# A decoder layer in split fp32: copies, sums, loads and stores of the hidden work put at other places in the engines' orders

## The chip, the cores and the metric

The kernel runs on one core of one Trainium2 chip. The core has TensorE (PE in the profile; its weight loads are PEld), VectorE (DVE), ScalarE (ACT), GpSimd (POOL) and SyncE (SP), and 16 DMA engines that move what SP and POOL issue here. The metric is the device time of one execution in microseconds. A time is given as the median of the executions shown.

## The reference, cut to what matters

One post-norm layer, 1024 tokens (S), width 2048, everything float32:

```
h = x @ w_in + b_in
q, k, v, g_attn, u_pool, g_pool = split(h)
a = banded_sink_attention(q, k, v, ...) * silu(g_attn)        # 16 heads, window 128
b = multiscale_pool(u_pool, w_pool, pool_scale) * silu(g_pool)  # trailing means of 2, 4, 8, 16
mix = concat([a, b]) @ w_out
ple = sigmoid(x @ w_gate_ple) * (p_i @ w_ple)
out = layer_norm(sqrt(2) * x + mix + ple, gain, bias)
```

## The kernel before, in words

**Products.** All activations are kept transposed, channels on partitions and tokens along the row. Each float32 operand is split into a high and a low part, `hi` and `lo`, and a product is the sum of hi·hi (L182), hi·lo (L183) and lo·hi (L184). A weight job makes two output blocks of 128 channels over half of the contraction. It is done after Strassen and Winograd, with seven products p1 to p7 in place of eight; their moving operands are the quarters `b11`, `b21`, `b22` of the activations and the sums `t1` to `t4` of quarters, each in a high (`t1h`) and a low (`t1l`) part. One product is 12 matmuls of 128x128 on 128x512: four slices of the contraction, three matmuls each. A product is one *tick* of the kernel's clock.

**Around a product.** SP loads the raw weights (`raw<-in_win`, L139). DVE forms sums of them (`s<-raw`, `raw<-raw,raw`, L125), ACT casts the high part (`wh`, L736), DVE subtracts to get the low part (`wl`, L125). PE leaves the product in a PSUM bank: `qa` or `qb` with two buffers each for a job by itself, `sc` and others for jobs side by side. ACT copies the first product of a quarter into the SBUF buffer of the output block, `part` (L402), DVE adds the others (`part<-part,qb`, L125); both free the bank for a later product. A second half of the contraction adds the first half's result to `part` by an accumulating DMA that POOL issues (L415: `part<-h`, `part<-g`), and some ticks later the block's outcome is worked out (`finished`, `done`).

**Stages**, from the trace of before: the qkv projection's first half with, in the *Head*, early products of the PLE weights ("per-layer embedding") between (to about 120 us); the other first halves with the attention heads woven in (to about 685); the second halves, first the pooling inputs `u` and gates, then the PLE gate `wgate`, then the gates of attention, the last two jobs side by side (to about 1125); the output projection (to about 1280); the same with its columns' mean taken out, for 768 tokens with products of 128x384 (to about 1402); the last 256 tokens without Strassen (to about 1455); the norm's end.

**What sets the order.** The program is written by a Python class. `after(n, fn)` runs `fn` n ticks later; `later(n, fn)` does the same and asks that its instructions be put behind those last issued (`issue_after`). A scheduler with priorities then fixes one order for each engine. Each engine runs its own order strictly: an instruction that waits holds all behind it. SP's loads and stores stand in one order too, and so do POOL's.

**What the change touches.**

- `ple_half` (L778), the PLE products in the Head: eight small groups of matmuls into the banks `tr` and `pv` (one buffer each), then two copies by ACT into `ple_out` (through `copy`, L736; the trace names the buffer `b22h`). `in_turn` asks that copies come behind the one before, once `turn["ACT"]` is set. `early` (L1152) places these halves in the first group.
- `set_from`'s `s2` (L317), which makes the sums `t1`, `t2` of the Head on DVE (`two<-two,two`, 128x1024).
- `set_kept`'s `step` (L344): splits an operand that was kept from the first stage, four pieces, and fetches the one after the next.
- `pool_sums` (L356): from four loaded quarters of the pooled channels (`s<-cc`, 256 KB each) DVE makes `t1`, `t3`, `t2`, `t4` (`s<-s,s`), which POOL stores for the output projection. Four such steps lie in the stage of `wgate`.
- `pool_u` (L704): fetch and split of the pooling's map. `embed_w` (L812): fetch and split of a block of `w_ple`; its high parts are the casts at L153.
- `gate_ahead` (L661) loads the stored attention result of a block (`s<-pre`, two of 256 KB); `gate_attn` (L664) takes the silu on ACT (L666), multiplies by those on DVE (`part<-s,part`), and stores the outcome to `cc` through POOL (`aside`, L144). Four jobs: two by themselves (`s3[-4]`, `s3[-3]`), the last two side by side.
- `job.wait`: the ticks between a block's accumulating DMA and its `done`. In the stage of 768 tokens `done` runs `norm_square`: ACT squares (L921), sums for the norm on PE (L930, L937).
- `norm_scale` (L940; ACT at L954) and `norm_out`, the norm of the 768 tokens, during the last stage.

Code that is quoted below has the line numbers of before. In the changed kernel L736 is L758, L402 is L420, L415 is L433, L666 is L684 and L834 is L857.

Of the kernel before, what the change touches and what calls it, by code (L numbers as in the profile page):

```python
# [64 lines left out]
class Layer:  # L65
# [203 lines left out]
    def set_from(self, get, F, keep=None, first=None, by=None):  # L269

        nc = self.nc
        r = {}

        def fetch(u, part=None):
            h, k = int(u[2]) - 1, 2 * (int(u[1]) - 1)
            if not part:
                r[u] = [self.two() for _ in range(2)]
            for i, t in enumerate(r[u]):
                src = get(h, k + i)
                if part is None:  # L280
                    (by or (nc.sync if first else nc.scalar)).dma_start(out=t, in_=src)
                elif i == 0 and part < 2:
                    self.load(t[:, part], src[:, part])
                elif i == 1 and part == 2:
                    self.load(t, src)

        def sub(u, a, b, place):
            out = []
            for k in range(2):
                o = r[place][k] if place else self.two()  # L290
                self.tt(o, r[a][k], r[b][k], ALU.subtract)
                if keep:
                    self.load(keep[u][k], o)
                out.append(o)
            r[u] = out

        split = lambda u: self.split_unit(u, r[u])

        def begin():
            self.F = F  # L300
            if first:
                first(fetch, r)
                return
            for i, u in enumerate(("b11", "b21", "b12", "b22")):
# [12 lines left out]
        def s2():  # L317
            split("t1")
            sub("t2", "b22", "t1", None if keep else "t1")

        def s3():
            split("t2")
            sub("t3", "b22", "b12", "b12")

        def s4():
            split("t3")
            sub("t4", "b21", "t2", "b21")

        return [begin, s0, s1, s2, s3, s4, lambda: split("b22"), lambda: split("t4")]

    def set_kept(self, get, keep):

        r = {}

        def fetch(i):
            if i < 7:
                u = UNITS[BESIDE[i]]
                h, k = int(u[2:] or 1) - 1, 2 * (int(u[1]) - 1)
                r[u] = []
                for n in range(2):  # L340
                    src = keep[u][n] if u in keep else get(h, k + n)
                    r[u] += [self.fetch(src[:, m]) for m in range(2)]

        def step(i):  # L344
            u = UNITS[BESIDE[i]]
            self.split_unit(u, r.pop(u))
            fetch(i + 2)

        def begin():
            self.F = T  # L350
            fetch(0)
            fetch(1)

        return [begin] + [lambda i=i: step(i) for i in range(7)]

    def pool_sums(self, i, m, keep):  # L356

        at = [(4 + i, 0), (4 + i, 1), (6 + i, 0), (6 + i, 1)]
        r = []

        def make():
            b11, b12, b21, b22 = r
            self.tt(b11, b12, b11, ALU.subtract)
            self.tt(b12, b22, b12, ALU.subtract)
            self.tt(b22, b22, b11, ALU.subtract)
            self.tt(b21, b21, b22, ALU.subtract)
            for u, t in (("t1", b11), ("t3", b12), ("t2", b22), ("t4", b21)):
                self.aside(keep[u][i][:, m], t)

        self.after(2, lambda: r.extend(self.fetch(self.cc[k][:, m, h * T : h * T + T]) for k, h in at))  # L370
        self.later(4, make)

    def set_by_twos(self, get, keep):

# [289 lines left out]
    def gate_attn(self, j, c):  # L664
        nc = self.nc
        nc.scalar.activation(c, c, AF.Silu, bias=self.c(C_BIN + GA0 + j))  # L666
        for h, pre in enumerate(self.got.pop(("ga", j))):
            self.tt(c[:, h], pre, c[:, h], ALU.mult)
        self.aside(self.cc[j // 2][:, j % 2], c.rearrange("p h t -> p (h t)"))

    def gate_pool(self, j, c):
        nc = self.nc
# [4 lines left out]
    def pool_u(self, j, c):  # L677
# [23 lines left out]
        self.diff[j] = out  # L701
        if j % 2:
            f = slice((g % 2) * T, (g % 2) * T + T)
            self.after(4, lambda: self.got.update({("wp", g): self.fetch(self.wpool[g // 2][:, f])}))  # L704
            self.later(8, lambda: self.got.update({("wp", g): self.split(self.got["wp", g])}))
            late = 3 if g == 1 else 0
            self.after(6 + late, lambda: self.got.update({("sg", g): [[self.fetch(self.sgp[2 * g + e][:, h * T : h * T + T]) for e in range(2)] for h in range(2)]}))
            self.later(10 + late // 2, lambda: self.mix(g))
# [69 lines left out]
    def ple_half(self, n, h, tags):  # L778
# [13 lines left out]
        for b in range(2):  # L792
            if h:
                self.aside(self.ple[2 * i + b], self.ple_out[(2 * n + b) % 4].rearrange("p h t -> p (h t)"))

    def embed_in(self, r=None):
        if not r:
# [14 lines left out]
    def embed_w(self, i):  # L812
# [2 lines left out]

        if i not in EARLY:
            r = self.fetch(self.wple[i // 2][:, (i % 2) * T : (i % 2) * T + T])
            self.later(2, lambda: make(r))

    def embed(self, j, c):  # L820
        nc = self.nc
# [166 lines left out]
    def run(self):  # L988
# [47 lines left out]
        def consume(w):  # L1036
            def done(b, c):
# [4 lines left out]
                elif b >= U0:  # L1042
                    self.pool_u(b - U0, c)
                else:
                    self.gate_attn(b - GA0, c)
            return done

        def jobs(todo, half, first, done, tokens=2 * T, ahead=None):
# [4 lines left out]
        s2 += jobs(rest, 1, lambda w: None, lambda w: keep(store(w)))  # L1053
        s3 = jobs(rest, 0, lambda w: kept_part(store(w)), consume)
        for j in s3:
            j.wait = 3 if j in s3[-2:] else 4
            j.ahead = self.embed_ahead if j.w is wgate else (lambda b: self.gate_ahead(b - GA0)) if j is s3[-3] else None
        mixed = [(wout, *p) for p in pairs(0, 8)]
        centred = [(self.wc, *p) for p in pairs(4, 6) + pairs(0, 2)]
        s4 = jobs(mixed, 1, lambda w: kept_part(self.r), lambda w: lambda b, c: self.co_done(b, c))  # L1060
# [4 lines left out]
            j.filled = True  # L1065
        s6 = [Job(w, b0, b1, 0, None, lambda b, c: self.second_done(b, c), F2, plain=True) for w, b0, b1 in centred]
        s6[-1].mean = True
        for j in s4[-2:]:
            j.wait = 6
        self.add(*s1[:3])  # L1070
        self.add(*s1[3:])
# [134 lines left out]
        for i in range(n3):  # L1206
# [7 lines left out]
            if i == n3 - 2:  # L1214
# [202 lines left out]
```

## Time and profile before

| | us |
|---|---|
| median of 3 runs | 1468.27 (1466.94 to 1468.92) |
| the profiled execution's own time | 1470.93 |
| its span | 1469.2 |
| PE busy | 1437.4 (98%) |
| DVE busy | 1120.8 (76%) |
| ACT busy | 787.3 (54%) |
| POOL busy | 294.4 (20%) |
| DMA | mean 205 GB/s over the span, 301.35 MB |

The granted clock of TensorE is 0.996 of full speed over the span. A row of the timeline gives the start in us, the busy time in us, engine, source line, operation and tiles, and in brackets how long the engine was idle ahead of it and what ended that wait. In the trace SP's DMA queue is called SPq. Buffers that share a name share a row.

### The profile page before, as it was taken

To read this page: it belongs to the slowest core of one execution; us is meant where nothing else is said; L and a number is where in the kernel's file an instruction comes from. 1 tells how busy PE (TensorE), PEld (TensorE's weight loads), DVE (VectorE), ACT (ScalarE), POOL (GpSimd) and SP (SyncE) were. 2 spreads that over 40 slices of the span, in tenths; PEclk is the share of its full clock that TensorE was granted. 3 is DMA by queue.
4 is the path that set the end of the run, shared out by engine and by line. 5 is a ranking of instruction groups with operands and counts; after the bars stand their busy time and mean duration, and the time that the engine had idled before them with its cause. 6 is when DMAs were issued, how large, how long until landed. Compare 5 with 4: busy or idle time off the path is not lost. (4 is left out here: it accounts for less than half of the span.)

```text
span 1469.2 us, 20535 instructions
## 1 busy us (share of the span) xinstructions
PE 1437.4 (98%) x6930; PEld 1214.9 (83%) x6930; DVE 1120.8 (76%) x2031; ACT 787.3 (54%) x1564; POOL 294.4 (20%) x416
## 2 busy tenths in 40 slices
PE   9999999999999999999999999999999999999996
PEld 7788888888888888887887788788877788899996
DVE  6869578878788797888668785867678566987786
ACT  6546376565575665566545444333456333554475
POOL 1000203332233333223010111211011111111223
PEclk9999999999999999999999999999999999999998
DMA  9463875554456554557765669899698678595475
GB/s 354 173 241 117 244 216 177 178 167 151 138 179 213 188 172 165 186 180 265 191 190 149 166 179 320 260 288 275 189 335 278 184 179 232 134 263 124 120 243 200
DMA packets 109993, 301.35 MB, mean 205 GB/s; under 512 B 12544, under 2 KB 18048, under 8 KB 109888
## 3 DMA queue, kind: packets, MB, share of 16 engines
q1 hardware_dynamic: 84672, 217.46, 43.4%
q0 software_dynamic: 21888, 75.25, 21.2%
q10 hardware_dynamic: 3328, 7.34, 1.5%
q8 instruction: 54, 0.88, 0.2%
q14 instruction: 51, 0.42, 0.1%
HBM read 205.62 MB, written 94.37 MB: 204 GB/s over the span
## 5 line engine op out<-in xcount | busy, mean ns | idle before, releaser
L736 ACT CAST wh<-raw 128x512 fp32r<-128x512 f32 x428 | 263.9, 619 | 400.5 <-PE qa L183 125.6
L125 DVE TENSOR_TENSOR wl<-raw,wh 128x512 fp32r<-128x512 f32 x428 | 300.0, 704 | 102.7 <-ACT wh L736 97.6
L402 ACT COPY part<-qa 128x512 f32<-128x512 f32 (+1 forms) x180 | 103.7, 576 | 74.9 <-PE qa L184 74.4
L620 POOL TENSOR_SCALAR_AFFINE_SELECT s<-s 128x512 fp32r<-128x512 f32 x128 | 102.4, 812 | 132.0 <-ACT s L613 96.5
L125 DVE TENSOR_TENSOR part<-part,qb 128x512 f32<-128x512 f32 (+1 forms) x120 | 81.1, 676 | 44.7 <-PE qb L184 40.1
L182 PE MATMUL qa<-b11h,wh 128*128 128x512 f32 (+2 forms) x292 | 109.4, 375 | 0.4 <-ACT wh L736 0.4
L182 PE MATMUL qb<-b21h,wh 128*128 128x512 f32 (+2 forms) x292 | 109.3, 374 | 0.0
L184 PE MATMUL qa<-b11h,wl 128*128 128x512 f32 (+2 forms) x292 | 108.8, 373 | 0.0
L184 PE MATMUL qb<-b21h,wl 128*128 128x512 f32 (+2 forms) x292 | 108.8, 372 | 0.0
L183 PE MATMUL qa<-b11l,wh 128*128 128x512 f32 (+2 forms) x292 | 108.7, 372 | 0.0
L183 PE MATMUL qb<-b21l,wh 128*128 128x512 f32 (+2 forms) x292 | 108.6, 372 | 0.0
L182 PE MATMUL qb<-t1h,wh 128*128 128x512 f32 (+1 forms) x260 | 100.8, 388 | 3.4 <-DVE part L125 1.6
L182 PE MATMUL qa<-t2h,wh 128*128 128x512 f32 (+1 forms) x260 | 101.1, 389 | 3.0 <-ACT wh L736 1.8
L182 PE MATMUL qa<-t4h,wh 128*128 128x512 f32 (+1 forms) x260 | 100.7, 387 | 2.7 <-DVE part L125 2.7
L182 PE MATMUL qa<-t3h,wh 128*128 128x512 f32 (+1 forms) x260 | 100.6, 387 | 1.6 <-ACT part L402 1.6
L184 PE MATMUL qa<-t2h,wl 128*128 128x512 f32 (+1 forms) x260 | 100.1, 385 | 1.8 <-DVE wl L125 1.8
L182 PE MATMUL qb<-b22h,wh 128*128 128x512 f32 (+1 forms) x260 | 100.5, 386 | 0.5 <-ACT part L402 0.5
L183 PE MATMUL qa<-t3l,wh 128*128 128x512 f32 (+1 forms) x260 | 99.8, 384 | 0.0
L184 PE MATMUL qb<-t1h,wl 128*128 128x512 f32 (+1 forms) x260 | 99.7, 384 | 0.0
L184 PE MATMUL qa<-t4h,wl 128*128 128x512 f32 (+1 forms) x260 | 99.7, 384 | 0.0
L183 PE MATMUL qa<-t2l,wh 128*128 128x512 f32 (+1 forms) x260 | 99.7, 383 | 0.0
L184 PE MATMUL qb<-b22h,wl 128*128 128x512 f32 (+1 forms) x260 | 99.7, 383 | 0.0
(327 smaller groups left out, 3567.2 us busy)
## 6 DMA issues: line engine op xcount, KB each, us to landing
raw<-in_win SPq DMA_DIRECT2D x65, 512.0 KB, 4.3
h<-part SPq DMA_DIRECT2D x34, 512.0 KB, 2.9
part<-h POOLq DMA_DIRECT2D x34, 512.0 KB, 6.6
cw<-in_wout SPq DMA_DIRECT2D x64, 256.0 KB, 3.0
raw<-in_wgate SPq DMA_DIRECT2D x32, 512.0 KB, 4.4
raw<-wc SPq DMA_DIRECT2D x32, 512.0 KB, 4.3
s<-in_x SPq DMA_DIRECT2D x44, 256.0 KB, 5.9
wc<-cw SPq DMA_DIRECT2D x32, 256.0 KB, 2.4
```

Source lines behind the costliest of these rows:

```text
L125: return (eng or self.nc.vector).tensor_tensor(out=out, in0=a, in1=b, op=op)
L182: mm(ps, wh, xh, start=start, stop=False, skip_group_check=True)
L183: mm(ps, wh, xl, start=False, stop=False, skip_group_check=True)
L184: return mm(ps, wl, xh, start=False, stop=stop, skip_group_check=True)
L402: self.mark("ACT", self.nc.scalar.copy(out=dst, in_=ps))
L620: nc.gpsimd.affine_select(out=o4, in_=a4, pattern=[[0, 4], [sign, P]], compare_op=ALU.is_ge, fill=0.0, base=0 if side else -1, channel_mul ...
L736: ins = self.nc.scalar.copy(out=out, in_=a)
```

## The change

It consists of these parts, in the order of the diff:

- Head: the sum `t2` is made two ticks later, by `later`; in `early` the copies of one half are no longer tied to those before (`turn["ACT"]` is dropped at (2, 1) and set again at (2, 0) from `ple_half`'s return value).
- `set_kept`: from the second step on, two of the four pieces are split one tick later.
- `pool_sums`: `later(4)` becomes two halves at `later(7)` and `later(8)`.
- `pool_u`: the fetch one tick sooner, the split one later. `embed_w`: the split at `later(4)` for `later(2)`.
- Gates: for the jobs `s3[-4]` and `s3[-3]` the loads of `pre` are placed by hand 1, 1, 5 and 6 ticks after the begin of the stage's last part, `wait` is 5 for 4, and the outcome is stored by SP one tick after it is made (`soon`), where POOL stored it at once.
- The squares of the stage of 768 tokens (but for its last two jobs): `wait` 6 for 4. `norm_scale` and `norm_out`: one tick later.

```
         def s2():
             split("t1")
-            sub("t2", "b22", "t1", None if keep else "t1")
+            if first:
+                self.later(2, lambda: sub("t2", "b22", "t1", None))
+            else:
+                sub("t2", "b22", "t1", None if keep else "t1")
...
-            self.split_unit(u, r.pop(u))
-            fetch(i + 2)
+            pieces = r.pop(u)
+            self.split_unit(u, [])
+            for n in range(2):
+                self.split_part(u, n, pieces[n])
+
+            def rest():
+                for n in range(2, 4):
+                    self.split_part(u, n, pieces[n])
+                fetch(i + 2)
+
+            if i:
+                self.after(1, rest)
+            else:
+                rest()
...
         self.after(2, lambda: r.extend(self.fetch(self.cc[k][:, m, h * T : h * T + T]) for k, h in at))
-        self.later(4, make)
+        for second in range(2):
+            self.later(7 + second, lambda second=second: make(second))
...
-        self.aside(self.cc[j // 2][:, j % 2], c.rearrange("p h t -> p (h t)"))
+        store = lambda by: by(self.cc[j // 2][:, j % 2], c.rearrange("p h t -> p (h t)"))
+        if soon:
+            self.after(1, lambda: store(self.load))
+        else:
+            store(self.aside)
...
-            self.after(4, lambda: self.got.update({("wp", g): self.fetch(self.wpool[g // 2][:, f])}))
-            self.later(8, lambda: self.got.update({("wp", g): self.split(self.got["wp", g])}))
+            self.after(3, lambda: self.got.update({("wp", g): self.fetch(self.wpool[g // 2][:, f])}))
+            self.later(9, lambda: self.got.update({("wp", g): self.split(self.got["wp", g])}))
...
-            self.later(2, lambda: make(r))
+            self.later(4, lambda: make(r))
...
-            j.wait = 3 if j in s3[-2:] else 4
-            j.ahead = self.embed_ahead if j.w is wgate else (lambda b: self.gate_ahead(b - GA0)) if j is s3[-3] else None
+            j.wait = 3 if j in s3[-2:] else 5 if j in s3[-4:-2] else 4
+            j.ahead = self.embed_ahead if j.w is wgate else None
...
-        for j in s4[-2:]:
+        for j in s4[-2:] + s5[:-2]:
             j.wait = 6
...
+            if at == (2, 1):
+                self.turn.pop("ACT")
             if at in turn:
-                self.ple_half(*turn[at], (("tr", 1), ("pv", 1)))
+                out = self.ple_half(*turn[at], (("tr", 1), ("pv", 1)))
+                if at == (2, 0):
+                    self.turn["ACT"] = out
...
-                for b in s3[-4].b:
-                    self.after(1, lambda b=b: self.gate_ahead(b - GA0))
+                for n, b in enumerate(s3[-4].b + s3[-3].b):
+                    self.after((1, 1, 5, 6)[n], lambda b=b: self.gate_ahead(b - GA0))
...
-        self.later(3, lambda: self.norm_scale(one, 2))
+        self.later(3, lambda: self.norm_scale(one, 3))
         for j in range(NB):
-            self.later(6 + 18 * j // 16, lambda j=j: self.norm_out(one, j))
+            self.later(7 + 17 * j // 16, lambda j=j: self.norm_out(one, j))
```

First place: ScalarE in the Head, where the copies `b22h<-tr` and `b22h<-pv` free the banks of the PLE products, `t2h` is the cast of a sum for a later operand, and `wh` are weights' high parts. Before:

```order
L736 CAST t1h_521<-two_309 128x1024
L736 CAST t2h_614<-two_527 128x1024
L736 CAST wh_557<-s_208_552 128x512
L736 CAST t2h_614<-two_530 128x1024
L736 COPY b22h_341<-tr_598 128x512
L736 COPY b22h_341<-pv_599 128x512
L736 CAST wh_580<-s_212_575 128x512
L736 CAST wh_624<-raw_293 128x512
L736 CAST wh_660<-raw_295 128x512
L402 COPY part_452<-qb_628 128x512
L736 COPY b22h_341<-tr_642 128x512
```

After:

```order
L758 CAST t1h_521<-two_309 128x1024
L758 CAST wh_551<-s_206_546 128x512
L758 COPY b22h_341<-tr_598 128x512
L758 COPY b22h_341<-pv_599 128x512
L758 CAST t2h_614<-two_569 128x1024
L758 CAST wh_580<-s_212_575 128x512
L758 CAST t2h_614<-two_572 128x1024
L758 CAST wh_624<-raw_293 128x512
L420 COPY part_452<-qb_628 128x512
L758 CAST wh_660<-raw_295 128x512
L758 COPY b22h_341<-tr_642 128x512
```

Both casts of `t2h` moved behind the copies of the first PLE half (`tr_598`, `pv_599`), and one of them behind the cast `wh_580`; the copy of the next half (`tr_642`) still stands behind both.

Second place: VectorE in the stage of `wgate`, around the first step of the pooling's sums. `s_9165<-s_9119,s_9164` is the low part of a `w_ple` block, `s_9168`, `s_9170`, `s_9172` and `s_9174` (`s_9164`, `s_9166` and so on after) are the four loaded quarters, and the additions `part<-part,qb` and `part<-part,qa` free banks. Before:

```order
L125 TENSOR_TENSOR part_9124<-part_9124,qb_9150 128x512
L125 TENSOR_TENSOR s_9165<-s_9119,s_9164 128x512
L125 TENSOR_TENSOR wl_9177<-raw_8652,wh_9176 128x512
L125 TENSOR_TENSOR wl_9200<-raw_8809,wh_9199 128x512
L125 TENSOR_TENSOR s_9168<-s_9170,s_9168 128x512
L125 TENSOR_TENSOR part_8957<-part_8957,s_9106 128x512
L834 SCALAR_TENSOR_TENSOR part_8957<-s_9102,part_8957 128x512
L125 TENSOR_TENSOR s_9170<-s_9174,s_9170 128x512
L125 TENSOR_TENSOR wl_9230<-raw_8833,wh_9229 128x512
L125 TENSOR_TENSOR s_9174<-s_9174,s_9168 128x512
L125 TENSOR_TENSOR s_9172<-s_9172,s_9174 128x512
L125 TENSOR_TENSOR part_9125<-part_9125,qa_9130 128x512
```

After:

```order
L125 TENSOR_TENSOR part_9124<-part_9124,qb_9150 128x512
L125 TENSOR_TENSOR wl_9173<-raw_8652,wh_9172 128x512
L125 TENSOR_TENSOR wl_9196<-raw_8809,wh_9195 128x512
L125 TENSOR_TENSOR part_8957<-part_8957,s_9106 128x512
L857 SCALAR_TENSOR_TENSOR part_8957<-s_9102,part_8957 128x512
L125 TENSOR_TENSOR wl_9222<-raw_8833,wh_9221 128x512
L125 TENSOR_TENSOR s_9216<-s_9119,s_9215 128x512
L125 TENSOR_TENSOR part_9125<-part_9125,qa_9130 128x512
...
L125 TENSOR_TENSOR s_9164<-s_9166,s_9164 128x512
L125 TENSOR_TENSOR raw_8833<-raw_8833 128x512
L125 TENSOR_TENSOR wl_9268<-raw_8833,wh_9267 128x512
L125 TENSOR_TENSOR e_9295<-s_9077,e_9294 128x512
```

The first sum of quarters (`s_9168<-s_9170,s_9168` before, `s_9164<-s_9166,s_9164` after) now stands ten rows behind the addition out of `qa` (`part_9125<-part_9125,qa_9130`); before, it stood seven rows ahead of it.

Third place: SP's queue at the gates of attention. `s<-pre` are the gates' inputs, `two<-pt` and `two<-cc` operands of the next stage, `raw` weights, `cc_236` and `cc_237` the outcome of the two single jobs. Before:

```order
L139 DMA raw_10544<-in_wout 128x1024
L139 DMA two_10580<-pt_252 128x1024
L139 DMA two_10582<-pt_253 128x1024
L139 DMA s_10602<-pre_156 128x512
L139 DMA s_10604<-pre_156 128x512
L139 DMA s_10607<-pre_157 128x512
L139 DMA s_10609<-pre_157 128x512
L139 DMA s_10778<-pre_158 128x512
```

After:

```order
L139 DMA raw_10536<-in_wout 128x1024
L139 DMA s_10561<-pre_156 128x512
L139 DMA s_10563<-pre_156 128x512
L139 DMA cc_236<-part_10290 128x1024
L139 DMA cc_236<-part_10291 128x1024
L139 DMA s_10584<-pre_157 128x512
L139 DMA s_10586<-pre_157 128x512
L139 DMA two_10588<-pt_252 128x1024
L139 DMA two_10590<-pt_253 128x1024
L139 DMA s_10778<-pre_158 128x512
```

The inputs of blocks 156 and 157 moved ahead of the loads of `pt`, and the stores of `cc_236`, which stood in POOL's queue, now stand between them; those of `cc_237` stand ten rows behind them in the same queue, ahead of `two<-pt_256`.

More of the change, by code (lines that the diff above doesn't have):

```diff
@@ L359, in pool_sums, with make @@
         r = []
-        def make():
+        def make(second):
             b11, b12, b21, b22 = r
[L363 to L367, printed above, removed]
+            if second:
+                self.tt(b22, b22, b11, ALU.subtract)
+                self.tt(b21, b21, b22, ALU.subtract)
+            else:
+                self.tt(b11, b12, b11, ALU.subtract)
+                self.tt(b12, b22, b12, ALU.subtract)
+            for u, t in (("t2", b22), ("t4", b21)) if second else (("t1", b11), ("t3", b12)):
                 self.aside(keep[u][i][:, m], t)
         self.after(2, lambda: r.extend(self.fetch(self.cc[k][:, m, h * T : h * T + T]) for k, h in at))
-        self.later(4, make)
+        for second in range(2):
+            self.later(7 + second, lambda second=second: make(second))
     def set_by_twos(self, get, keep):
@@ L662, in gate_ahead, with gate_attn @@
         self.got["ga", j] = [self.fetch(self.pre[j][:, h * T : h * T + T]) for h in range(2)]
-    def gate_attn(self, j, c):
+    def gate_attn(self, j, c, soon):
         nc = self.nc
@@ L668, in gate_attn @@
             self.tt(c[:, h], pre, c[:, h], ALU.mult)
-        self.aside(self.cc[j // 2][:, j % 2], c.rearrange("p h t -> p (h t)"))
+        store = lambda by: by(self.cc[j // 2][:, j % 2], c.rearrange("p h t -> p (h t)"))
+        if soon:
+            self.after(1, lambda: store(self.load))
+        else:
+            store(self.aside)
     def gate_pool(self, j, c):
@@ L794, in ple_half @@
                 self.aside(self.ple[2 * i + b], self.ple_out[(2 * n + b) % 4].rearrange("p h t -> p (h t)"))
+        return out.ins
     def embed_in(self, r=None):
@@ L1044, in done @@
                 else:
-                    self.gate_attn(b - GA0, c)
+                    self.gate_attn(b - GA0, c, b in s3[-4].b + s3[-3].b)
             return done
```

## The prediction

> **What bounds the kernel now.** I read the page first, then the waits of PE, then PE's timeline wait by wait, and for each wait the timelines of ACT and DVE around it. The page's first row and the two longest kinds of wait:
>
> ```profile
> PE 1437.4 (98%) x6930; PEld 1214.9 (83%) x6930; DVE 1120.8 (76%) x2031; ACT 787.3 (54%) x1564; POOL 294.4 (20%) x416
> ```
> ```profile
> PE qa L182 <- ACT part L402: 2.7, 5, 1.2
> PE qa L182 <- DVE part L125: 2.7, 4, 1.7
> ```
>
> PE is the bound. The change takes no matmul away, so all that it can gain is waiting, and few waits are longer than 0.3 us. What one costs shows in the Head:
>
> ```profile
> 38.28 0.39 PE L183 MATMUL qb<-t1l,wh 128*128 128x512 f32 x1
> 38.51 0.39 PE L184 MATMUL qb<-t1h,wl 128*128 128x512 f32 x1
> 40.34 0.50 PE L182 MATMUL tr<-t4h,t3h 128*128 128x512 f32 x1 [1.44 <-ACT b22h L736]
> 40.68 0.40 PE L183 MATMUL tr<-t4l,t3h 128*128 128x512 f32 x1
> ```
>
> Matmuls start 0.23 apart; around this wait the starts are 1.83 and 0.34 apart, so it costs 1.83 + 0.34 - 0.46 = 1.71, the idle time plus 0.27. I price every wait so. A product of 12 matmuls takes 12 x 0.23 = 2.7.
>
> **The change part by part.** *Head.* The wait just shown is for the copy that empties `tr`; the product before it waited for an addition that stood behind the first sum for `t2` on DVE:
>
> ```profile
> 35.93 0.47 PE L182 MATMUL qb<-t1h,wh 128*128 128x512 f32 x1 [0.38 <-DVE part L125]
> ```
> ```profile
> 38.75 1.04 ACT L736 CAST t2h<-two 128x1024 fp32r<-128x1024 f32 x1 [1.64 <-DVE two L125]
> 39.70 0.58 ACT L736 COPY b22h<-tr 128x512 f32<-128x512 f32 x1
> 40.18 0.59 ACT L736 COPY b22h<-pv 128x512 f32<-128x512 f32 x1
> 41.22 0.62 ACT L736 CAST wh<-s 128x512 fp32r<-128x512 f32 x1 [0.45 <-DVE s L125]
> 41.74 1.14 ACT L736 CAST wh<-raw 128x512 fp32r<-128x512 f32 x2
> 42.79 0.57 ACT L402 COPY part<-qb 128x512 f32<-128x512 f32 x1
> 43.26 0.58 ACT L736 COPY b22h<-tr 128x512 f32<-128x512 f32 x1
> ```
> ```profile
> 40.44 0.69 DVE L125 TENSOR_TENSOR s<-raw 128x512 f32<-128x512 f32 x1
> ```
>
> With the copy ahead of both casts of `t2h`, both waits go: 0.65 + 1.71 = 2.4. But the casts now stand ahead of the next copy. Before, the next PLE half would start a half and a product after 40.34, at about 40.34 + 0.1 + 2 x 2.7 = 45.9; with 2.4 taken off, PE wants `tr` at 43.5. On DVE the sum at 40.44 keeps its place (as many rows of the same kind stand ahead of it), ending at 41.1; behind it ACT has a `wh` (0.52 to the next start), `t2h` (0.95), `wh` (0.52), the copy of `part` (0.47), `wh` (0.52) and the copy of `tr` (0.58): it ends at 41.2 + 3.6 = 44.8. So a wait of 1.3 takes the place of those removed, and the Head gains 2.4 - 1.4 = 1.0. Ends: 0 (PE waits as long, one product later) and 2.4 (the copy is in time).
>
> *`set_kept`.* PE's wait ends when a cast of `wh` and an addition end together:
>
> ```profile
> 695.60 0.46 PE L182 MATMUL qb<-t1h,wh 128*128 128x512 f32 x1 [0.89 <-ACT wh L736]
> ```
> ```profile
> 694.77 0.68 DVE L125 TENSOR_TENSOR part<-part,qb 128x512 f32<-128x512 f32 x1
> ```
>
> Each stands one instruction earlier on its engine, which is 0.6: gain 0.6, from 0 to 0.9. Where the same split comes elsewhere, and for `pool_u`'s pieces, no wait of PE stands behind it: nothing; PE's cover is the products already split, and uncovered each would cost one such 0.6.
>
> *Pooling's sums and `w_ple`'s splits.* DVE holds additions behind sums whose quarters have not landed (the rows of DVE), and PE waits four times there, once for ACT behind a sigmoid (the last row):
>
> ```profile
> 916.67 0.69 DVE L125 TENSOR_TENSOR s<-s,s 128x512 f32<-128x512 f32 x1 [4.22 <-DMA s<-cc]
> ...
> 942.87 2.15 DVE L125 TENSOR_TENSOR s<-s,s 128x512 f32<-128x512 f32 x3 [1.22 <-DMA s<-cc]
> ```
> ```profile
> 917.19 0.50 PE L182 MATMUL qb<-b22h,wh 128*128 128x512 f32 x1 [0.46 <-ACT part L402]
> ...
> 921.88 0.50 PE L182 MATMUL qa<-t4h,wh 128*128 128x512 f32 x1 [1.65 <-DVE part L125]
> ...
> 930.57 0.50 PE L182 MATMUL qa<-t2h,wh 128*128 128x512 f32 x1 [0.24 <-ACT part L402]
> ...
> 946.27 0.51 PE L182 MATMUL sc<-e,s 128*128 128x512 f32 x1 [1.68 <-DVE part L125]
> ```
> ```profile
> 915.08 1.06 ACT L822 ACTIVATE part<-part 128x1024 f32<-128x1024 f32 x1 [1.92 <-DMA part<-g]
> ```
>
> The sums come three and four ticks later, 8 to 11 us, which is longer than the wait of 4.22. The waits at 921.88 and 946.27 go (1.92 + 1.95), and that at 930.57, behind casts that are moved, too (0.51): 4.4. The first, 0.46, stays: its copy stands behind a sigmoid that waits for the accumulating DMA `part<-g`, which the change does not bring forward. What is late next is that DMA. On POOL the stores of the sums now come behind later accumulations, and on SP the loads of the quarters keep their tick, so the slots of four quarters are held three ticks longer and loads of `s<-in_x` behind them in SP's order may wait. I find no user on PE within a product of them: 0, with 2.0 to lose (one such wait more) and 0.7 to gain.
>
> *Gates.*
>
> ```profile
> 1077.29 2.66 DVE L125 TENSOR_TENSOR part<-s,part 128x512 f32<-128x512 f32 x4 [3.62 <-DMA s<-pre]
> ...
> 1096.08 0.69 DVE L125 TENSOR_TENSOR part<-s,part 128x512 f32<-128x512 f32 x1 [0.59 <-DMA s<-pre]
> ```
> ```profile
> 1081.20 0.50 PE L182 MATMUL qa<-t4h,wh 128*128 128x512 f32 x1 [0.54 <-DVE part L125]
> ...
> 1099.07 0.49 PE L184 MATMUL qa<-t2h,wl 128*128 128x512 f32 x1 [0.69 <-DVE wl L125]
> ...
> 1108.65 0.50 PE L182 MATMUL qa<-t3h,wh 128*128 128x512 f32 x1 [1.21 <-ACT part L402]
> ```
> ```profile
> 1105.63 0.59 ACT L402 COPY part<-qb 128x512 f32<-128x512 f32 x1 [2.52 <-DMA cc<-part]
> 1106.12 1.99 ACT L736 CAST t1h<-two 128x1024 fp32r<-128x1024 f32 x2
> 1108.01 0.59 ACT L402 COPY part<-qa 128x512 f32<-128x512 f32 x1
> ```
> ```profile
> two<-pt SPq DMA_DIRECT2D x7, 512.0 KB, 8.0
> ...
> cc<-part POOLq DMA_DIRECT2D x4, 512.0 KB, 8.2
> r<-part SPq DMA_DIRECT2D x2, 512.0 KB, 4.4
> ```
>
> With `s<-pre` there, and the silus a tick later, DVE does not stop at 1077, and the first two waits go: 0.81 + 0.96. The third stays, since it hangs on a store: the copy of `part` needs the buffer that `cc` is written from. The multiplications then end at about 1096.1 (the second without its wait of 0.59); SP stores at that time, where POOL stored an instruction later. Landing takes 8.2: 1104.3. Behind it ACT has the copy (0.59), one `t1h` (0.95), a `wh` (0.62) and the copy of `part` out of `qa` (0.59): PE goes on at about 1107.0 instead of 1108.65. The stage's gain is then 1.7; at least 0.8 (the first wait alone) and at most 3.3 (all three). A store on SP also holds SP's queue until DVE is done: `two<-pt` stands behind it. Its first user is ACT's `t2h`, several products later. POOL's accumulations `part<-h`, which stood behind those stores, now wait for their own data alone; I count nothing for it, as the silu of a tick later finds them landed either way.
>
> The Trainium skill says in DMA: Bandwidth & Descriptors, section "Issuing engines are not separate DMA queues", that DMAs of all issuers run on the same engines, and another issuer saves only the small time of initiation; the trace agrees (POOL's 8.2, SP's 8.0). A rule that speaks for more is in SBUF — State Buffer, section "SBUF: two separate sides": DMAs issued by GpSimd starve for descriptors while VectorE works in a two-port mode, those from SP do not. By it the store would land like `r<-part`, at about 1100.5, and the third wait would go as well.
>
> *Squares and norm.* Those waits in the stage of 768 tokens are:
>
> ```profile
> 1381.42 0.44 PE L182 MATMUL qb<-t1h,wh 128*128 128x384 f32 x1 [0.82 <-DVE d L125]
> ```
> ```profile
> 1411.56 1.56 PE L937 MATMUL sc<-q,ones 128*128 128x512 f32 x4 [0.35 <-ACT q L954]
> ```
> ```profile
> 1420.00:1430.00 10.00, 10.00 (x17) 1.00 0.97 320
> ```
>
> Around the first, DVE and ACT have the same order after as before: it stays, 0. The second goes (0.62), but DVE is busy without a gap behind it (10.00 of 10.00) and feeds the last stage, so part of it comes back: 0.3, from -0.5 to 0.9.
>
> The sum is 1.0 + 0.6 + 4.4 + 1.7 + 0.3 = 8.0. Against the profiled execution's own 1470.93 (span 1469.2, the rest lies around it): 1462.9. The median, 1468.27, is 2.66 lower: **1460.3**.
>
> **The rivals.** *No change to speak of: DMA sets these stages.*
>
> ```profile
> 920.00:960.00 40.00, 36.42 (x157) 1.00 0.85 262
> ```
>
> DMA is busy 0.85 of this window. If landing sets the pace there, PE waits the same elsewhere, for `part<-g` or `cc`; only Head, `set_kept` and tail remain, 1.0 + 0.6 + 0.3 = 1.9: 1466.4. For it: every stop above ends with a DMA. Against: PE waited 3.6 of 40, where a bound would show in each window, and the moved sums are needed a stage later.
>
> *Slower: the accumulations come late.* The quarters' loads (1 MB for each of four steps; at the window's 262 GB/s 3.8 us of all DMA engines) now share that time with `part<-g`, since the sums' stores move away. If all of it delays the accumulation, the sigmoid at L822, which already waited 1.92, holds ACT and the copy of `part` behind it 3.8 longer, four times: 15.2 - 8.0 = 7.2 slower, 1475; with a share of 0.8, 4 x 3.0 - 8.0 = 4: **1472**. It decides from 2.8 for each step (8.0 + 2.9 = 10.9 in all). For it: PE's 0.46 at 917.19 is that chain, with no slack. Against: the loads were at the same tick before.
>
> *More: no new wait in the Head, and the store lands early.* 2.4 + 0.6 + 4.4 + 3.3 + 0.9 = 11.6: 1456.7. It needs `t2h` not ahead of the copy, which the order shows, and a landing near 4.4; the skill's rule on descriptors would give its second half. Against: POOL's and SP's landings of equal size agree within 0.2.
>
> **How the numbers follow.** Forecast 0.58; no change 0.20; more 0.12; slower 0.10. A difference of 0.2% (2.9 us) is about the least that a measurement of this kernel can tell from none, so "same" is 1465.3 to 1471.2. Forecast and "more" are faster, with a fifth of "no change": 0.74. Same: the rest of it, and some of the slow case at a small delay: 0.18. Slower 0.08. The forecast's own bounds (8.0 less 1.0, 0.6, 2.0, 0.9 and 0.8, so 2.7 at the worst; more by 1.4, 0.3, 0.7, 1.6 and 0.6, so 12.6 at the best) give 1455.7 to 1465.6. To hold the time 8 times in 10 the range takes in "no change" above, and "more" lies in it as it is: 1455.5 to 1466.5, which leaves out the slower rival and the far ends of the others.
>
> **What would show it.** Right: no wait at the `tr` product after the first `t1h`, and one near 1.3 at the next half; none of over 0.3 on `qa<-t4h` and `sc<-e,s` around 920 and 945; the one at 917 still there; `s<-pre` no longer releasing DVE at 1077; a wait of about 1 to 2 us on `qa<-t3h` near 1100; the one for `d` at 1381 still there. Wrong: PE's time between 890 and 950 not shorter by 3, or sigmoids that wait much longer for `part<-g`; `cc<-part` landing in 4 to 5.

## The result, and the profile after

| | before | changed |
|---|---|---|
| median of 19 runs each, us | 1468.96 (1466.19 to 1471.72) | 1465.3 (1462.69 to 1468.16) |
| ratio, with its 95% interval | | 0.9973 [0.9966, 0.9981] |
| profiled execution: own time / span, us | 1470.93 / 1469.2 | 1465.53 / 1463.8 |

The kernel became faster by 3.7 us of median, where 8.0 was forecast. The time lies in the stated range and the gain has the forecast's sign, but it is less than half as large. The two profiled executions are 5.4 us of span apart; before's had a time 2 us above its median, the changed kernel's 0.2.

The waits view of PE, changed kernel, its first three rows. Those for `part` have shrunk (2.7 and 2.7 before, 2.3 and 0.5 now); that of `qb` for a cast `wh` has grown from 1.3 to 2.2, with one of 1.7 in it:

```profile
PE qa L182 <- ACT wh L758: 2.8, 4, 1.5
PE qa L182 <- ACT part L420: 2.3, 4, 1.4
PE qb L182 <- ACT wh L758: 2.2, 2, 1.7
```

The timeline of PE, changed kernel, at the places of the prediction's list of signs:

```profile
44.89 0.50 PE L182 MATMUL tr<-t4h,t3h 128*128 128x512 f32 x1 [0.89 <-ACT b22h L758]
...
695.38 0.47 PE L182 MATMUL qb<-t1h,wh 128*128 128x512 f32 x1 [0.29 <-ACT t2h L758]
...
1100.85 0.50 PE L182 MATMUL qa<-t3h,wh 128*128 128x512 f32 x1 [1.42 <-ACT part L420]
...
1130.10 0.47 PE L182 MATMUL qb<-t1h,wh 128*128 128x512 f32 x1 [1.75 <-ACT wh L758]
...
1136.02 0.50 PE L182 MATMUL qb<-t1h,wh 128*128 128x512 f32 x1 [1.37 <-DVE part L125]
...
1376.20 0.44 PE L182 MATMUL qb<-t1h,wh 128*128 128x384 f32 x1 [0.82 <-DVE d L125]
```

Four of the six are as foreseen: the Head's wait one PLE half later, the `set_kept` wait down from 0.89 to 0.29, the store's wait still there, that for `d` unchanged. The fifth row, 1.37 at 1136, is not on the prediction's list, but before had a wait at the same matmul:

```profile
1141.68 0.50 PE L182 MATMUL qb<-t1h,wh 128*128 128x512 f32 x1 [1.23 <-DVE part L125]
```

Between 900 and 950 no wait is left. So the one at 917 is gone as well, which the prediction kept: the sigmoid ahead of it waited 1.02 for `part<-g` here, 1.92 before. The windows of the changed kernel (window, length, PE busy with matmuls, granted clock, DMA share, GB/s):

```profile
920.00:960.00 40.00, 40.00 (x177) 1.00 1.00 314
1080.00:1120.00 40.00, 38.58 (x170) 1.00 0.98 326
```

In the first of them PE busy went from 36.42 to 40.00 of 40 while DMA's share rose from 0.85 to 1.00. So transfers did not set the pace of the pooling's sums. The fourth row of the timeline is new: 1.75 at 1130, behind the gates. ACT there, changed kernel:

```profile
1126.27 1.16 ACT L684 ACTIVATE part<-part,cst 128x1024 f32<-128x1024 f32 x1 [3.93 <-DMA part<-h]
1129.44 0.62 ACT L758 CAST wh<-s 128x512 fp32r<-128x512 f32 x1 [2.02 <-DVE s L125]
```

A silu of the last two gate jobs waits for its accumulating transfer; DVE's multiplications wait for the silu, a sum of weights stands behind those on DVE, the cast `wh` behind the sum, and PE behind the cast. The instructions stood in that order before, too, and the silu waited 1.65. What is late is the transfer. POOL issued it at 1116.07, and it landed just ahead of 1126.27, 10.2 later; before, the silu went on 8.1 after the issue (1123.87 to 1131.93):

```profile
1116.07 0.88 POOL L433 DMA_DIRECT2D part<-h  x1 [2.05 <-ACT part L420]
```

SP's queue says what ran beside it. Changed kernel:

```profile
1102.65 0.59 SPq L139 DMA_DIRECT2D s<-pre  x1
1103.34 4.93 SPq L139 DMA_DIRECT2D raw<-in_wout  x3
1108.32 0.90 SPq L139 DMA_DIRECT2D s<-pre  x2
1109.27 0.90 SPq L139 DMA_DIRECT2D two<-pt  x2
1110.21 0.91 SPq L139 DMA_DIRECT2D s<-pre  x2
```

Before:

```profile
1080.53 14.28 SPq L139 DMA_DIRECT2D s<-pre  x7
...
1098.05 1.00 SPq L139 DMA_DIRECT2D s<-pre  x2
...
1110.20 3.68 SPq L139 DMA_DIRECT2D raw<-in_wout  x3
```

Before, all gates' inputs were under way by 1099, eleven us ahead of the weights. Now five of the last ones (1.25 MB) come among the weights or behind them, in the 10 us ahead of the accumulations. The order shows why: the store of the second single gate job, `cc_237`, stands in SP's queue now, so SP waits there for DVE's multiplications. Five loads of blocks 159 to 161 come behind it, and also behind `two<-pt`, `two<-cc` and a weight, which SP issued between 1096 and 1102.

### The profile page after: what moved, and what is told of

It reads as the page before. It is cut to its first block, busy times and chain, and to the rows that moved or that the text cites. A ratio compares the mean times of both kernels' runs of the same rounds, so it can differ in the third digit from the quotient of the medians.

```text
span 1463.8 us, 20540 instructions
## 1 busy us (share of the span) xinstructions
PE 1436.6 (98%) x6930; PEld 1214.8 (83%) x6930; DVE 1120.4 (77%) x2031; ACT 787.5 (54%) x1564; POOL 291.9 (20%) x412
## 5 line engine op out<-in xcount | busy, mean ns | idle before, releaser
L183 PE MATMUL qa<-t4l,wh 128*128 128x512 f32 (+1 forms) x260 | 99.7, 383 | 0.0
```

The costliest lines, as they stand in the source:

```text
L183: mm(ps, wh, xl, start=False, stop=False, skip_group_check=True)
```

## The experiments

**Theory P**: the gates' part gains what was forecast, and the store on SP gives it back, because it pushes the loads of the last gates' inputs into the time of the accumulating transfers. **Theory Q**: the stage is paced by its transfers as a whole, so whatever PE gains is given back at the next one. Beside them stood the suspicion that one execution's waits are not the usual ones.

To compare many profiles I count matmuls from the start of the trace and take the time from one to another. The stretches: start to matmul 240 (the Head), 240 to 4200 (qkv, attention heads, first second halves), 4200 to 4400 (the four pooling sums), 4400 to 5080 (to behind the wait on the store), 5080 to 5230 (into the output projection), 5230 to the end of the span.

| profile | Head | to 4200 | sums | gates | behind gates | rest |
|---|---|---|---|---|---|---|
| before | 59.10 | 842.51 | 50.75 | 158.69 | 35.53 | 322.66 |
| before_again | 59.54 | 840.90 | 49.43 | 158.74 | 36.07 | 322.44 |
| changed | 58.44 | 842.59 | 45.60 | 156.62 | 37.67 | 322.90 |
| after_again | 57.83 | 843.04 | 45.69 | 156.23 | 38.10 | 322.31 |
| pre_early | 57.94 | 841.21 | 45.60 | 156.44 | 34.74 | 321.98 |
| no_pre | 58.76 | 843.73 | 45.62 | 156.38 | 35.28 | 322.54 |
| store_pool | 57.76 | 841.07 | 45.74 | 160.18 | 35.11 | 323.24 |
| only_sums | 58.66 | 842.48 | 46.24 | 159.26 | 35.74 | 322.51 |
| only_gates | 58.23 | 841.89 | 48.58 | 156.08 | 38.17 | 323.32 |
| no_gates | 58.96 | 843.72 | 45.63 | 158.74 | 35.61 | 323.02 |
| gates_early | 58.31 | 840.39 | 49.39 | 158.05 | 36.55 | 321.53 |
| only_head | 58.42 | 843.76 | 48.03 | 158.60 | 35.96 | 322.67 |
| pe_soon0 | 58.00 | 842.71 | 45.88 | 156.54 | 35.15 | 322.11 |
| pe_no_squares | 57.54 | 841.48 | 45.79 | 156.60 | 34.64 | 322.08 |

Not all that a stretch gains or loses is waiting. In three profiles the granted clock was halved for a while between 1095 and 1140: in store_pool from 1099.7 for 6.8 us, in after_again from 1130.2 for 3.4, in gates_early from 1104.6 for 3.4. Half of that time is lost, so by this estimate after_again holds 1.7 of it behind the gates, gates_early 0.8 at the gates and 0.9 behind them, and store_pool 2.5 and 0.9. The other profiles hold none in these two stretches.

**before_again.** No edit.

> The kernel before, profiled once more. Theory A (the chance of one execution): the profiled execution of before, at 1470.93, held waits on loads that a usual execution does not hold, and that is why the pair of profiles is 5.4 us apart and the medians 3.66. Then the waits at sc<-e,s near 946 (1.68) and at qa<-t4h near 921 (1.65) come out smaller here, together by 1 us or more, and the time is nearer to 1469. Theory B (the waits are a fixed part of the order): both are within 0.3 us of the first profile, and what differs between executions lies elsewhere.

One execution took 1468.83. The same two waits of PE:

```profile
919.86 0.50 PE L182 MATMUL qa<-t4h,wh 128*128 128x512 f32 x1 [1.25 <-DVE part L125]
...
943.80 0.50 PE L182 MATMUL sc<-e,s 128*128 128x512 f32 x1 [1.22 <-DVE part L125]
```

They are 0.40 and 0.46 smaller, 0.86 together, and the third (0.46 at 917) is not there: the stretch is 1.3 shorter. Theory A's number, 1 us at these two, was missed by little, and its point holds: five profiles with the old sums took 50.75, 49.43, 48.58, 49.39 and 48.03, mean 49.24, and the execution that I predicted from was the worst of them.

**after_again.** No edit.

> The changed kernel, profiled once more. Theory C (the new waits belong to the new order): the wait for the cast wh ahead of qb<-t1h near 1130 (1.75) is there again within 0.4 us, released by a silu that waits 3 us or more for part<-h. Theory D (chance): it is below 0.8. The small waits for the scores near 637 (0.39 and 0.21), behind a load of cw that landed 5.3 us after its issue, are expected by either to be different, since nothing in the order changed there.

1464.93 in one execution. Theory C: the wait is there and longer.

```profile
1130.04 0.59 PE L182 MATMUL qb<-t1h,wh 128*128 128x512 f32 x1 [2.15 <-ACT wh L758]
```

The Head's wait at `tr` was absent in this profile, though.

**pre_early.**

```
-                    self.after(14 + 2 * n, lambda b=b: self.gate_ahead(b - GA0))
+                    self.after(11 + 1 * n, lambda b=b: self.gate_ahead(b - GA0))
```

> The changed kernel with the loads of the last four gates' inputs put 3 to 6 ticks sooner, so that those of blocks 159 to 161 stand ahead of the weights' loads in SP's queue. Theory P (placement: these loads, 1 MB, run beside the accumulating transfers and delay them): the wait near 1130 falls from 1.75 to below 0.5, the silu's wait for part<-h from 3.9 to below 2, and the time by about 2 us against the changed kernel, to a ratio of 0.996 to before. Theory Q (the stage is paced by its transfers as a whole): the wait near 1130 stays above 1.2, or comes back as a longer one at qa<-t3h near 1100, and the time stays at a ratio of 0.9973.

Measured: 0.9950 [0.9936, 0.9963], 1461.2 us, an interval that does not meet the changed kernel's. SP's queue, with the last four gates' inputs ahead of the weights, and PE's timeline:

```profile
1095.49 1.95 SPq L139 DMA_DIRECT2D s<-pre  x4
1098.97 0.33 SPq L139 DMA_DIRECT2D raw<-in_wout  x1
```
```profile
1098.76 0.50 PE L182 MATMUL qa<-t3h,wh 128*128 128x512 f32 x1 [1.21 <-ACT part L420]
...
1131.02 0.50 PE L182 MATMUL qb<-t1h,wh 128*128 128x512 f32 x1 [0.45 <-DVE part L125]
```

The third accumulation let its silu go on 7.3 after the issue (1113.99 to 1121.28), instead of 10.2. The wait for `wh` is gone, and the next one, 1.37 at 1136, is down to 0.45; before had it at 1.23, so here the order is better than before's and not only rid of the loss (34.74 behind the gates, 35.53 before). The wait on the store did not grow. Theory P, and Theory Q falls. This kernel beats both.

**no_pre.**

```
-                    self.after(14 + 2 * n, lambda b=b: self.gate_ahead(b - GA0))
+                    if n < 2:
+                        self.after(14 + 2 * n, lambda b=b: self.gate_ahead(b - GA0))
...
-        for h, pre in enumerate(self.got.pop(("ga", j))):
+        for h, pre in enumerate(self.got.pop(("ga", j), None) or [c[:, 0], c[:, 1]]):
```

> The changed kernel without the loads of the gates' inputs of the last two blocks (160 and 161, four loads of 256 KB): their gates multiply by themselves, so that part of the output is not computed. Theory P: the third accumulating transfer lands 6 to 8 us after its issue instead of 10.2, and the wait near 1130 goes below 0.5. Theory Q: with 1 MB less of some 5 MB in that time the wait falls by a fifth to a half only. Theory R (the new wait has nothing to do with these loads): 1.75 as before.

1464.03 in one execution, whose Head was 0.9 slower than after_again's. The wait for `wh` near 1130 is gone, and the silu went on 7.8 after the issue of its accumulation (1117.32 to 1125.13). The wait behind it is 0.98:

```profile
1134.88 0.50 PE L182 MATMUL qb<-t1h,wh 128*128 128x512 f32 x1 [0.98 <-DVE part L125]
```

The stretch behind the gates takes 35.28 instead of 37.67 and 38.10. So taking 1 MB away does to the wait for `wh` what placing it sooner does; Theories Q and R expected half of that wait or more to be left.

**store_pool.**

```
-            self.after(1, lambda: store(self.load))
+            self.after(1, lambda: store(self.aside))
```

> The changed kernel with one word back: the outcome of the two single gate jobs is stored by POOL (still one tick later), not by SP. In this order the loads of blocks 158 to 161 stand ahead of the weights' loads in SP's queue again, as before the change. Theory P1 (the store on SP is what pushed those loads back): the wait near 1130 (1.75 and 2.15 in two profiles) falls below 0.5, and the ratio to before is 0.995, as with the loads put sooner by hand. Theory P2 (the stores' own landing decides, and SP's is the better one): the wait at qa<-t3h near 1100 grows by 1 us or more, and the ratio stays at 0.997. By the descriptor rule weighed in the prediction the store from POOL would also land later than SP's 7.1; by the trace of before it lands within 0.5 of it.

0.9967 [0.9955, 0.9978]: not told apart from the changed kernel. Both theories got half. The wait near 1130 is gone and the stretch takes 35.11, so the store on SP is what pushed the loads back. But the wait on the store became the longest of the profile:

```profile
1100.31 0.79 PE L182 MATMUL qa<-t3h,wh 128*128 128x512 f32 x1 [2.94 <-ACT part L420]
```

It is not that POOL's store lands later. ACT went on at 1096.78 after an issue at 1089.30, 7.5 later; in the changed kernel it was 7.4 (1090.81 to 1098.26):

```profile
1089.30 0.56 POOL L144 DMA_DIRECT2D cc<-part  x1 [11.48 <-DVE part L125]
```
```profile
1096.78 0.59 ACT L420 COPY part<-qb 128x512 f32<-128x512 f32 x1 [2.83 <-DMA cc<-part]
1097.26 1.99 ACT L758 CAST t1h<-two 128x1024 fp32r<-128x1024 f32 x2
```

In this order both casts of `t1h` stand between the waiting copy and the one that PE needs, 1.9 us, where the changed kernel has one, 0.95. That explains about 1 of the 1.5 us that the wait grew by. The rest is the time of the issue: PE stopped 8.1 after it here (1089.30 to 1097.37) and 8.6 after it in the changed kernel (1090.81 to 1099.43). The gates' stretch is 3.6 longer than the changed kernel's, and the wait is not the larger part of that: the granted clock was halved at the end of it (window, length, PE busy, granted clock, DMA share, GB/s).

```profile
1099.70:1106.50 6.80, 6.19 (x15) 0.50 0.89 306
```

**only_sums** (the hunks of `pool_sums` and `embed_w` alone, on the kernel before).

> The kernel before with only the pooling's sums and the splits of w_ple later. By the prediction 4.4 us less, ratio 0.9970; by the second profile of before, whose waits at these places cost 0.8 us less, 3.5 to 4, ratio 0.9975. Rival (the time is given back at the gates, whose transfers pace them): under 2 us, ratio above 0.9985.

0.9973 [0.9963, 0.9983], 11 runs: the ratio of the whole change. The stretch of the sums took 46.24; over the nine profiles with the later sums the mean is 45.75, against 49.24: 3.5. Only the wait at 917 was left:

```profile
916.70 0.50 PE L182 MATMUL qb<-b22h,wh 128*128 128x512 f32 x1 [0.44 <-ACT part L405]
```

**only_gates** (the gates' hunks alone, on the kernel before).

> The kernel before with only the gates' part. Theory P1: 1.7 to 2 us gained from 1080 to 1110, and some 2 given back near 1135 by a wait for the cast wh behind the silu, so a ratio of 1.000 within 0.001. By the prediction, which saw no such wait, 0.9988.

1.000 [0.999, 1.001], 11 runs. PE's timeline holds the whole trade: the two first waits gone, that on the store 0.90, then the new one:

```profile
1102.39 0.50 PE L182 MATMUL qa<-t3h,wh 128*128 128x512 f32 x1 [0.90 <-ACT part L402]
...
1132.14 0.47 PE L182 MATMUL qb<-t1h,wh 128*128 128x512 f32 x1 [2.25 <-ACT wh L740]
```

Stretch of the gates 156.08 (old order: 158.69, 158.74, 159.26, 158.74, 158.60, mean 158.8), behind them 38.17 (old order: mean 35.8).

**no_gates** (the changed kernel without the gates' hunks).

> The changed kernel without the gates' part. Theory P1: the loss near 1130 is not there, and neither is the gain from 1080 to 1110, so the time is that of the changed kernel: ratio 0.997 to 0.9975. By the prediction it would be 1.7 us slower than the changed kernel: 0.9985.

0.9965 [0.9953, 0.9977]: as the changed kernel, or a little better, and without gain and loss at the gates (158.74, 35.61). As Theory P had it; the prediction's 0.9985 lies outside the interval.

**gates_early** (the gates' hunks and pre_early's line, on the kernel before).

> The kernel before with the gates' part of the change, and with the loads of the last four gates' inputs 3 to 6 ticks sooner. The gates' part alone measured 1.000. Theory P1 (what it gains from 1080 to 1110, 2 to 2.5 us, is lost again near 1130 through those loads): with them sooner the ratio is 0.9975 to 0.9985, and the wait for wh near 1130 (2.25 in the gates' part alone) is below 0.5. Rival (the gain of the loads put sooner needs the rest of the change): within 0.001 of 1.000.

0.9982 [0.9972, 0.9992], within P1's numbers. The wait near 1130 is gone. The profile is less kind than the time: the wait on the store is 2.13, and the gates' stretch at 158.05 shows little gain; 0.8 of it is the halved clock. The store there took 8.8 to land (issued at 1092.57, ACT on at 1101.37), with loads of gates' inputs issued just ahead of it and during it. The loads put sooner can thus cost some of the gain at the store; three profiles of the changed kernel with them (156.44, 156.54, 156.60) do not show it.

```profile
1103.01 0.50 PE L182 MATMUL qa<-t3h,wh 128*128 128x512 f32 x1 [2.13 <-ACT part L402]
```

**only_head** (the Head's hunks alone, on the kernel before).

> The kernel before with only the Head's part. By the prediction 1.0 us less, ratio 0.9993, with a wait of about 1.3 at the second tr<-t4h product in the first group; by the profiles of the changed kernel so far (that wait was 0.89, 1.55 and four times absent; start 0.34 to 1.34 earlier) 0.6 us, which the time cannot tell from none. Rival (the Head's gain does not reach the end): the product near 57 starts as late as in before.

1.0003 [0.9992, 1.0014]. The wait was there, 0.66, and the Head took 58.42:

```profile
44.90 0.50 PE L182 MATMUL tr<-t4h,t3h 128*128 128x512 f32 x1 [0.66 <-ACT b22h L739]
```

Over the five profiles without the Head's part the mean is 58.77, over the nine with it 58.18: 0.6. That this reaches the end isn't shown: the following stretch took between 840.39 and 843.76 in 14 profiles, and only_head's is the longest.

**pe_soon0** (pre_early, and `store(self.load)` at once instead of one tick later).

> The changed kernel with the last four gates' loads sooner, and the single gates' outcome stored by SP at once instead of one tick later; the store of the second job then stands ahead of the second load of block 159. Theory S (the wait at qa<-t3h near 1099, 1.21, hangs on when that store is issued): the store is issued about 0.5 to 1 us sooner and the wait falls as much; ratio 0.9945 to 0.995. Rival (its landing decides, and that does not move): the wait stays within 0.3 of 1.21, ratio 0.995.

0.9956 [0.9942, 0.997], and a wait of 1.33: the rival's number, but not for its reason. The store was issued at 1090.77 against 1089.34 in pre_early, with PE later as well, so only about 0.4 sooner by the program's progress (1.4 later, with PE 1.8 later at matmul 4400). ACT went on 7.4 after it (1098.14), in pre_early 7.8 (1097.11), so that the waiting copy was 0.8 sooner in all. But in this order a cast of `t1h` (0.95) stands between that copy and the one that PE needs; in pre_early none does.

```profile
1100.73 0.50 PE L182 MATMUL qa<-t3h,wh 128*128 128x512 f32 x1 [1.33 <-ACT part L420]
```

**pe_no_squares** (pre_early with the hunks on `s5[:-2]`, `norm_scale` and `norm_out` undone).

> The changed kernel with the last four gates' loads sooner, but with the squares and the norm of the 768 tokens where they were before the change. By the prediction the squares do nothing and the norm's step 0.3 us: ratio 0.995 to 0.9955, the waits for wh and d near 1370 (0 to 0.55 and 0.82) there as before, and one of 0.35 at the sum of squares near 1400 back again. Rival (the later squares carry part of the gain): ratio above 0.996.

0.9952 [0.9939, 0.9964], as pre_early. The waits are the expected ones, 0.82 for `d` and 0.39 at the sum of squares, and the rest of the program is not longer (322.08). The squares and the norm's step do nothing that these runs can tell.

```profile
1370.59 0.44 PE L182 MATMUL qb<-t1h,wh 128*128 128x384 f32 x1 [0.82 <-DVE d L125]
...
1400.80 1.56 PE L960 MATMUL sc<-q,ones 128*128 128x512 f32 x4 [0.39 <-ACT q L977]
```

## Why the prediction came out half right

The direction was right, the size was not: 3.7 us for 8.0. By its own terms:

- **Head, 1.0 forecast, 0.6 found.** The mechanism is the one worked out. In the changed kernel's profile the copy of `tr` starts at 44.25 and takes 0.58, so it ends at 44.83; 44.8 was forecast, and PE waited 0.89. What the profile of before could not tell is that DVE's whole row of sums starts 0.4 to 1.1 sooner in some executions. Then that wait is absent, as in six of the nine profiles, and yet the Head gains 0.6 only, since before's Head varies as well (its wait of 1.44 at `tr` was 0.41 to 1.42 in the other four profiles with the old Head).
- **`set_kept`, 0.6 forecast.** The wait fell from 0.89 to 0.29 as forecast, and to 0.28 to 0.54 in six of the seven others with this part (0.90 in no_gates); the six profiles without it have 0.88 to 1.00. This part has no run of its own.
- **Sums, 4.4 forecast, 3.5 found.** All the waits are gone, 917's in eight of nine profiles as well, where the prediction said that it stays. The term was mis-sized: it was read from the one execution in which they were longest.
- **Gates, 1.7 forecast; 2.5 gained and 2.2 lost.** The gain is larger than forecast, and the wait on the store stayed as forecast (1.42, 1.03, 0.90). The step that failed is "A store on SP also holds SP's queue until DVE is done: `two<-pt` stands behind it." I named one thing that stands behind the store, and left out the loads of blocks 159 to 161, for which the order as quoted ahead of the prediction already shows that the queue had changed. They were pushed into the accumulations' time, where the third `part<-h` held its silu until 10.2 after the issue (8.1 before), PE waited 1.75 more, and the part came out at nothing (1.000 by itself). pre_early, no_pre and store_pool each undo that push in a way of its own, and each removes the wait. A second sentence failed without a cost that shows: "the silu of a tick later finds them landed either way". The second silu of the later single job still waited 2.75 for `part<-h`, 2.13 before.
- **Squares and norm, 0.3 forecast, 0 found.** Mean of the last stretch: 322.5 without and 322.6 with the later squares, seven profiles each. The wait at the sum of squares is gone as forecast (0.35 before, 0.39 back in pe_no_squares), but the time does not show it.

Head 0.6, sums 3.5, gates 2.5 - 2.2, squares 0: 4.4, and the medians say 3.7. What is left is in the long middle stretch, where the mean is 0.4 longer with the change (eight profiles, 842.4) than without it (six, 842.0), though it includes the 0.6 of `set_kept`. Single profiles scatter over 3.4 us there, so the sum of it is not told from chance. One place of it can be seen: from matmul 2660 to 2880 (near 605 to 650) the five profiles without the Head's part take 44.2 to 44.7, mean 44.5, and the nine with it 44.2 to 46.2, mean 45.4. DVE waits there for a load of a weight that is centred, 1.1 to 1.5 in the five and 1.3 to 3.0 in the nine; the change doesn't touch that load. The timeline of DVE, before and then changed:

```profile
630.62 0.69 DVE L125 TENSOR_TENSOR cw<-cw,wmean 128x512 f32<-128x512 f32 x1 [1.31 <-DMA cw<-in_wout]
```
```profile
630.95 0.69 DVE L125 TENSOR_TENSOR cw<-cw,wmean 128x512 f32<-128x512 f32 x1 [3.02 <-DMA cw<-in_wout]
```

It was issued at 626.90 and at 625.68, and DVE went on 3.7 and 5.3 later. So on the mean the Head's gain is waited away here. That PE being ahead is what makes the load late is not shown.

Of the rivals, "DMA sets these stages" fell at the sums (PE busy 40.00 of 40) and had something at the gates: landing times decide there, but by the order of the loads, not by their sum. "Accumulations come late" was the right mechanism at the wrong place. I priced it for the sums, where the sigmoid waited less for `part<-g` (1.02 for 1.92), and not for the gates, where `part<-h` came later. POOL's store landed within 7.5 and SP's within 7.4. The Trainium skill's rule on descriptors (SBUF — State Buffer, "SBUF: two separate sides") holds for a VectorE in a two-port mode; the prediction took that condition for granted, and no run here shows it met, so these two numbers do not test the rule. The Trainium skill's rule that another issuer saves only the time of initiation (DMA: Bandwidth & Descriptors, "Issuing engines are not separate DMA queues") agrees with them. It doesn't cover what happened: the issuer made no difference to the store and a large one to the loads behind it.

## What to carry to other kernels

When a store that waits for computed data moves into a queue of loads, list every load behind it, up to the next place where transfers are dense, and ask what those loads will then run beside. A gain that is read from waits on transfers should be sized from several executions, since one profile may be the one in which they are long. A part of a change that measures nothing can hold a gain and a loss of equal size: here 2.5 and 2.2, and moving one line kept the first without the second.

## What was not expected of the hardware

- The same transfer lands very differently by what runs beside it: `part<-h` of 512 KB took a median of 6.6 over the whole of before, and the silu that needs it went on 10.2 after the issue at the place above; for the 256 KB load of `cw` DVE went on 3.7 and 5.3 after the issue in two executions at the same place of the program.
- With a DMA share of 1.00 for 40 us, PE did not wait once in the changed kernel (40.00 of 40): a full share is no sign by itself that transfers are the bound.
- The two profiles of before differ by 1.6 us in the middle stretch and by 1.3 at the sums, while before's medians in four sets of runs lie within 1.6 us (1468.27 to 1469.8).
- A wait of PE can cost more than itself. Close to waits of 2.94, 2.15 and 2.13 the granted clock was halved for 6.8, 3.4 and 3.4 us (store_pool, after_again, gates_early); close to one of 2.25 it was not (only_gates). What decides it is not shown.
